# State-space steps between the projections: TensorE in the order of the source, two heads alternating on the column halves

## The chip, the cores and the metric

One core of a Trainium2 chip runs the kernel. The metric is the device time of one execution in microseconds; the median of three runs is given. TensorE does the matmuls, VectorE and ScalarE the elementwise work, SyncE issues the loads and stores. GpSimd does nothing here.

## What is computed

One layer of a hybrid block on 256 latent tokens and 256 context tokens of width 2048, in fp32. A normalised and modulated input goes through one wide projection. Its columns feed a state-space mixer (SSD: 32 heads of 64 in 4 groups, state 128, chunks of 128 tokens, both directions), a recurrent mixer (RG-LRU) and gates; an output projection and a gated FFN follow. The change touches the state-space mixer:

```python
def ssd_scan(x, dt, A, B, C, h0):
    xdt, Bc, a_cum, states, chunk_decay = _ssd_chunks(x, dt, A, B)
    entering, final = _carry_states(states, chunk_decay, h0)
    ...
    Lmat = jnp.exp(jnp.where(lower, seg, -jnp.inf))
    CB = jnp.einsum('bcign,bcjgn->bcijg', Cc, Bc)
    y_diag = jnp.einsum('bcijg,bcijge,bcjgep->bcigep', CB, Lmat, xdt)
    y_off = jnp.einsum('bcign,bcige,bcgepn->bcigep', Cc, jnp.exp(a_cum), entering)
    return (y_diag + y_off).reshape(b_, L, G, E, P), final
```

It is done forward and backward and summed; the context gives the states that enter the latent scan. Then `y * silu(z)`, a norm and the projection `w_out_ssd`.

## The kernel before

A *job* is one projection of 128 output columns: its weight comes in parts of 8 k-tiles (512 KB each, `load`), ScalarE rounds a part to `wh`, VectorE takes the rest `wl = raw - wh` (`parts`, L165 and L166), and `product` (L171 on) accumulates `wh` and `wl` against the split activations in one of three PSUM banks named `ps`. "both" jobs cover latent and context tokens (three matmuls of 512 columns per k-tile, 48 in all, L177 to L179), "lat" jobs the latent tokens (48 of 256 columns, L181 to L183), "packed" jobs two matmuls per k-tile (512 and 256 columns, L195 and L196). Four buffers each of raw weights, `wh` and `wl` go round, and `forward` keeps them filled. After its last matmul a job calls `evac`, whose first step is a ScalarE copy out of `ps` (L393, L426, L256).

`run` walks through a list of jobs. After each it issues one step of `ada_rest` (two loads of 512 KB and a VectorE product each, L415 and L416), where there are some, and takes one or two entries off the queue `bg` and calls them.

The list `jobs` has first the step sizes, the recurrent mixer's projections and gates (34 jobs), then for each of four groups B, C and four x projections (`bs_evac`, `cs_evac`, `xs_evac`: a convolution over four taps on ScalarE and VectorE), then eight gate jobs. Sixteen z jobs and sixteen yr jobs follow. When a group's last x is there, `ssd_group(g)` puts ten entries on `bg`: the three Silus; `products` (transposes pB of B into Bt, and pC = B.C, masked into U and L); transposes px of x with weighted copies xw; context states (p0); carried states (p1); and four units (u, c), each four heads on one chunk of 128 tokens. A unit loads AC, makes the operands E, G and CE on ScalarE and VectorE, and then does for each pair of heads t and each head e of the pair three matmuls py with 64 weight columns (L742 to L744): head e = 0 writes PSUM partitions 0 to 63, e = 1 partitions 64 to 127. `dve` adds the skip term into yt (L746), and y goes to DRAM for the z jobs. State-space PSUM tiles come from three banks named `ssd`; two more, `lru`, belong to the recurrent mixer and a few sums.

The order of the instructions on each engine is set by a planner that simulates the program and takes what is ready by priority. Only the first stage fixes TensorE's and SyncE's order by hand. So around the groups TensorE's matmuls of different jobs and of the state-space steps stand as the planner mixed them. An fp32 matmul shows as two passes in the records.

Of the kernel before, what the change touches and what calls it, by code (L numbers as in the profile page):

```python
# [14 lines left out]
P = 128  # L15
# [39 lines left out]
def hybrid_block(  # L55
# [152 lines left out]
    bg, loaded, n_parts = deque(), deque(), [0]  # L208

    def run(jobs, after=(), ada=(), every=1, start=0):  # L210
# [54 lines left out]
    def rstd_of(ps, n, name):  # L265
        r = tp.tile([P, n], F32, tag="rstd", name=name, bufs=1)
        fn(r, ps[:, :n], AF.Sqrt, bias=epsb[:, 0:1], scale=1.0 / D)
        dve.reciprocal(r, r)
        return r
# [14 lines left out]
    r1 = rstd_of(ssq, 2 * T, "r1")  # L284
# [311 lines left out]
    def start_ssd():  # L596
# [6 lines left out]
        held["ld"] = ap_stack.enter_context(tc.tile_pool(name="ld", bufs=5))  # L603
# [3 lines left out]
    def bs_evac(g):  # L607
        def f(ps):
            if g == 0:
                start_ssd()  # L610
            gp = sd["gp"]
            B = sd["B"] = gp.tile([P, 2 * T], F32, tag="B", name="B", bufs=1)
            conv(ps, B.rearrange("p (s t) -> p s t", s=2), col("cw", 4 * (16 + g), 4), col("cb", 16 + g), 2)
        return f

    def cs_evac(g):
        def f(ps):
            gp = sd["gp"]
            Cm = sd["C"] = gp.tile([P, T], F32, tag="C", name="Cm", bufs=2)
            conv(ps, Cm.unsqueeze(1), col("cw", 4 * (20 + g), 4), col("cb", 20 + g), 1)  # L620
            sd["XS"] = gp.tile([P, 4, 2 * T], F32, tag="XS", name="XS", bufs=2)
        return f

    def xs_evac(g, t):
        def f(ps):
            i = 4 * g + t
            conv(ps, sd["XS"][:, t, :].rearrange("p (s t) -> p s t", s=2), col("cw", 4 * i, 4), col("cb", i), 2)
            if t == 3:
                bg.extend(ssd_group(g))
        return f  # L630

    def ssd_group(g):
# [15 lines left out]
        def products():  # L648

            pb = ssd_ps("pB")  # L650
            for q in range(4):
                pe.transpose(pb[:, q * P:q * P + P], B[:, q * P:q * P + P], ident)
            Bt = st["Bt"] = gp.tile([P, 4, P], F32, tag="Bt", name="Bt")
            act.copy(Bt.rearrange("p a b -> p (a b)"), pb)

            pc = ssd_ps("pC")
# [9 lines left out]
        def tokens(qs):  # L666

            def weighted(ps, blk, d):
                o = gp.tile([P, 4 * P], F32, tag="xw", name="xw", bufs=3)
                dve.tensor_tensor(heads(o), heads(ps), head_scale(wt[:, blk], d), ALU.mult)  # L670
                return o

            def f():
                for q in qs:
                    px = ssd_ps("px")
                    for t in range(4):
                        pe.transpose(px[:, t * P:t * P + P], XS[:, t, q * P:q * P + P], ident)
                    if q < 2:
                        o = st["xt", q] = gp.tile([P, 4 * P], F32, tag="xt", name="xt", bufs=2)
                        act.copy(o, px)  # L680
                        st["xl", q] = weighted(px, 4, q)
                    else:
                        for d in range(2):
                            st["xc", d, q - 2] = weighted(px, 3 + q, d)
            return f

        def context_states():
            for d in range(2):
                p0 = ssd_ps("p0")
# [5 lines left out]
                st["S", d, d] = s0  # L695

        def carried_states():
            for d in range(2):
                p1 = ssd_ps("p1")
                pe.matmul(p1, st["Bt"][:, d, :], st["xl", d], start=True, stop=True)  # L700
                s1 = gp.tile([P, 4 * P], F32, tag="s1", name="s1", bufs=2)
                dve.tensor_tensor(heads(s1), heads(st["S", d, d]), head_scale(dec, d), ALU.mult)
                dve.tensor_tensor(s1, p1, s1, ALU.add)
                st["S", 1 - d, d] = s1

        def unit(u, c):

            def f():
                if c == 0:
                    for t in range(2):  # L710
                        st["y", t] = gp.tile([P, T], F32, tag="yt", name="yt", bufs=2)
                U, L = st["U"], st["L"]
                h0 = 8 * g + 4 * u
                cs = slice(c * P, c * P + P)
                AC = gp.tile([P, 2, 4, P], F32, tag="AC", name="AC", bufs=2)
                side.dma_start(AC.rearrange("p d h i -> p d (h i)"),
                                    acD[c, :, h0:h0 + 4, :].rearrange("d h i -> d (h i)").partition_broadcast(P))
                CE = gp.tile([P, 2, 4, P], F32, tag="CE", name="CE", bufs=1)
                fn(CE, AC, AF.Exp)
                CEv = CE.rearrange("p d h i -> p (d h) i")  # L720
                dve.tensor_tensor(CEv, CEv, Cm[:, cs].unsqueeze(1).broadcast_to([P, 8, P]), ALU.mult)
                E = gp.tile([P, 4, P], F32, tag="E", name="E", bufs=1)
                G = gp.tile([P, 4, P], F32, tag="G", name="G", bufs=1)
                for h in range(4):
# [3 lines left out]
                                             ALU.add, ALU.min)  # L728
                fn(E, E, AF.Exp)
                for h in range(4):  # L730
# [4 lines left out]
                dve.tensor_tensor(G, G, E, ALU.mult)  # L735
                for t in range(2):
                    py = ssd_ps("py")
                    for e in range(2):
                        h = 2 * t + e
                        xs = slice((4 * u + h) * 64, (4 * u + h) * 64 + 64)  # L740
                        o = py[64 * e:64 * e + 64, :P]
                        pe.matmul(o, st["xt", c][:, xs], G[:, h], start=True, stop=False)  # L742
                        pe.matmul(o, st["S", c, 0][:, xs], CE[:, 0, h], start=False, stop=False)
                        pe.matmul(o, st["S", c, 1][:, xs], CE[:, 1, h], start=False, stop=True)  # L744
                    i = 4 * g + 2 * u + t
                    dve.scalar_tensor_tensor(st["y", t][:, cs], XS[:, 2 * u + t, cs], col("dsk", i), py[:, :P],  # L746
                                             ALU.mult, ALU.add)
                    if c:
                        side.dma_start(yD[i], st["y", t])
            return f  # L750

        return ([silus, products, tokens((2, 3)), context_states, tokens((0, 1)), carried_states]
                + [unit(u, c) for u in range(2) for c in range(2)])

# [4 lines left out]
    jobs += gates_next(6)  # L759
    for g in range(NG):  # L760
        jobs.append(Job(w_bc[g], KT, "both", None, bs_evac(g)))
        jobs.append(Job(w_bc[4 + g], KT, "lat", None, cs_evac(g)))
        for t in range(4):
            jobs.append(Job(w_xs[4 * g + t], KT, "both", None, xs_evac(g, t)))
# [59 lines left out]
    run(jobs, after=z_jobs, ada=range(26), start=39)  # L824


    for k in range(KT):
        dve.tensor_copy(T1[:, k, T:], T2[:, k, :T].bitcast(F32))

    run(z_jobs, after=yr_jobs)  # L830
# [185 lines left out]
```

## Time and profile before

| | |
|---|---|
| median of three runs | 2035.52 us (2035.03 to 2035.86) |
| the profiled execution's own time | 2039.19 us |
| its span | 2037.4 us |
| TensorE matmuls busy | 1997.7 us, 98% |
| VectorE / ScalarE busy | 1436.5 us, 71% / 1084.1 us, 53% |
| mean granted TensorE clock | 0.994 of 2.4 GHz |
| HBM traffic | 438 MB, 215 GB/s over the span |

Matmuls are pipelined and their ends are modelled, so how long TensorE takes for something is read from the starts: the distance from one start to the next. In the rows below a timeline row is: start in us, length in us, engine, line, operation, output <- inputs, shapes and number of merged instructions; in square brackets what the engine waited for just before. Group 0 of the state-space work has its last projection at 496 us, the gate jobs begin near 737, the z jobs near 805, the yr jobs near 911.

### The profile page before, as it was taken

The page shows a single profiled execution, that of the slowest core. Times are in us where ns is not written, and L with a number is a line of the kernel's source. Part 1 is how long each engine was busy: PE and PEld are TensorE (multiplying, and loading weights), DVE is VectorE, ACT ScalarE, POOL GpSimd, SP SyncE. Part 2 cuts the span into 40 slices and gives each one's busy share as a digit, 9 for nine tenths or more (in the row PEclk, how much of TensorE's full clock was granted, in tenths as well). Part 3 has the DMA queues.
Part 4 walks back from the last instruction along what each step waited for, and adds up shares of the span by engine and source line. Part 5 has one row for each costly group of instructions (what it writes and reads, how often), then busy time and mean ns, then how long its engine had stood idle before and what let it go on. Part 6 is the DMA issues. An engine that isn't in the chain of part 4 may idle for free.

```text
span 2037.4 us, 30480 instructions
## 1 busy us (share of the span) xinstructions
PE 1997.7 (98%) x11633; PEld 1692.2 (83%) x11633; DVE 1436.5 (71%) x2148; ACT 1084.1 (53%) x1644; POOL 0.2 (0%) x4
## 2 busy tenths in 40 slices
PE   7999999999999999999999999999999999999997
PEld 4679888898777788888888888788888888888886
DVE  5467899985777788879896666766666665545554
ACT  4344888874453545755655544544444444544442
POOL 0000000000000000000000000000000000000000
PEclk9999999999999999999999999999999999999999
DMA  9984445464565668699996655577767765566663
GB/s 359 356 275 147 136 137 158 150 201 144 185 194 175 199 197 283 187 351 328 322 344 214 193 193 188 169 225 241 235 231 227 237 220 185 182 190 187 186 192 124
DMA packets 143266, 440.32 MB, mean 216 GB/s; under 512 B 17424, under 2 KB 36112, under 8 KB 142992
## 3 DMA queue, kind: packets, MB, share of 16 engines
q1 hardware_dynamic: 142752, 437.91, 66.2%
q8 instruction: 91, 1.49, 0.3%
q10 hardware_dynamic: 368, 0.47, 0.1%
q14 instruction: 55, 0.45, 0.1%
HBM read 427.77 MB, written 10.55 MB: 215 GB/s over the span
## 4 chain that ended last, share of the span: by engine, by line
PE 89%; DMA 4%; ACT 3%; DVE 2%; issue 1%; DVEq 0%; SPq 0%; ACTq 0%
PE ps L195 37%; PE ps L196 19%; PE ps L177 5%; PE ps L178 5%; PE ps L179 5%; PE ps L181 3%; PE ps L182 3%; PE ps L183 3%; DMA raw<-in_dram 1%; PE ps L342 1%; PE ps L343 1%; PE ps L344 1%; PE pa L295 1%; DMA wa<-in_dram 1%; DMA X<-in_dram 1%
## 5 line engine op out<-in xcount | busy, mean ns | idle before, releaser
L195 PE MATMUL ps<-T,wh 128*128 128x512 f32 x3332 | 1174.0, 397 | 7.0 <-DVE T L924 4.5
L166 DVE TENSOR_TENSOR wl<-raw,wh 128x1024 fp32r<-128x1024 f32 (+1 forms) x562 | 678.2, 1208 | 391.7 <-ACT wh L165 388.6
L165 ACT CAST wh<-raw 128x1024 fp32r<-128x1024 f32 (+1 forms) x562 | 582.0, 1038 | 677.8 <-issue 277.1
L196 PE MATMUL ps<-T,wl 128*128 128x256 f32 x3332 | 935.4, 281 | 0.8 <-DVE wl L166 0.8
L195 PEld LDWEIGHTS ps<-T,wh 128*128 128x128 f32 x3332 | 626.0, 188 | 158.8 <-issue 5.3
L196 PEld LDWEIGHTS ps<-T,wl 128*128 128x128 f32 x3332 | 629.6, 189 | 2.8 <-DVE wl L166 1.3
L416 DVE SCALAR_TENSOR_TENSOR rawa<-rawa,sc 128x1024 f32<-128x1024 f32 x128 | 156.5, 1222 | 76.6 <-DMA rawa<-in_dram 75.7
L177 PE MATMUL ps<-T,wh 128*128 128x512 f32 x464 | 186.0, 401 | 0.4 <-ACT gt L426 0.4
L178 PE MATMUL ps<-T,wh 128*128 128x512 f32 x464 | 185.2, 399 | 0.0
L179 PE MATMUL ps<-T,wl 128*128 128x512 f32 x464 | 184.2, 397 | 0.0
L182 PE MATMUL ps<-T,wh 128*128 128x256 f32 x576 | 165.4, 287 | 0.0
L183 PE MATMUL ps<-T,wl 128*128 128x256 f32 x576 | 164.8, 286 | 0.0
L181 PE MATMUL ps<-T,wh 128*128 128x256 f32 x576 | 164.3, 285 | 0.4 <-ACT gt L426 0.4
L181 PEld LDWEIGHTS ps<-T,wh 128*128 128x128 f32 x576 | 110.8, 192 | 4.2 <-issue 1.5
L183 PEld LDWEIGHTS ps<-T,wl 128*128 128x128 f32 x576 | 110.9, 193 | 2.8 <-issue 1.9
L182 PEld LDWEIGHTS ps<-T,wh 128*128 128x128 f32 x576 | 111.0, 193 | 2.6 <-issue 1.2
L177 PEld LDWEIGHTS ps<-T,wh 128*128 128x128 f32 x464 | 87.2, 188 | 22.8 <-issue 4.9
L179 PEld LDWEIGHTS ps<-T,wl 128*128 128x128 f32 x464 | 87.1, 188 | 21.5 <-issue 4.0
L178 PEld LDWEIGHTS ps<-T,wh 128*128 128x128 f32 x464 | 87.2, 188 | 21.4 <-issue 4.7
L106 ACT ACT_TABLE_LOAD x44 | 56.5, 1283 | 0.7
L336 DVE TENSOR_TENSOR wl<-raw,wh 128x896 fp32r<-128x896 f32 x16 | 17.5, 1092 | 45.7 <-ACT wh L335 45.7
L342 PE MATMUL ps<-T,wh 128*128 128x512 f32 x112 | 47.4, 423 | 0.0
(234 smaller groups left out, 1833.4 us busy)
## 6 DMA issues: line engine op xcount, KB each, us to landing
raw<-in_dram SPq DMA_DIRECT2D x546, 512.0 KB, 4.5
rawa<-in_dram SPq DMA_DIRECT2D x128, 512.0 KB, 4.8
wa<-in_dram SPq DMA_DIRECT2D x64, 512.0 KB, 7.6
AC<-acD SPq DMA_DIRECT2D x16, 512.0 KB, 6.2
raw<-in_dram SPq DMA_DIRECT2D x16, 448.0 KB, 7.9
raw<-in_dram SPq DMA_DIRECT2D x18, 256.0 KB, 2.7
X<-in_dram SPq DMA_DIRECT2D x8, 512.0 KB, 7.2
lw<-in_dram SPq DMA_DIRECT2D x16, 256.0 KB, 3.4
```

The costliest lines, as they stand in the source:

```text
L165: act.copy(h[:, :n], raw[:, :n])
L166: dve.tensor_sub(l[:, :n], raw[:, :n], h[:, :n].bitcast(F32))
L177: pe.matmul(ps, wh, T1[:, k, :], start=s, stop=False)
L178: pe.matmul(ps, wh, T2[:, k, :], start=False, stop=False)
L179: pe.matmul(ps, wl, T1[:, k, :], start=False, stop=e)
L181: pe.matmul(ps[:, :T], wh, T1[:, k, :T], start=s, stop=False)
L182: pe.matmul(ps[:, :T], wh, T2[:, k, :T], start=False, stop=False)
L183: pe.matmul(ps[:, :T], wl, T1[:, k, :T], start=False, stop=e)
L195: pe.matmul(ps, wh, a, start=s, stop=False, skip_group_check=True)
L196: pe.matmul(ps[:, T:], wl, a[:, :T], start=False, stop=e, skip_group_check=True)
L342: pe.matmul(ps0[n], h[:, n, :], T1[:, k, :], start=k == 0, stop=False)
L416: dve.scalar_tensor_tensor(rv, rv, 1.0, sc[:, h * 1024:h * 1024 + 1024], ALU.mult, ALU.mult, accum_out=MP[:, n, h:h + 1])
```

## The change

- TensorE's instructions from the first group's first job to the last z job stand in the order of the source (`manual_schedule` for PE). All other engines stay under the planner.
- A group's steps no longer queue in `bg`. Each gets a turn: `in_turn(n, f)` calls f after the n-th job from the group's last x on (that job is turn 0). For groups 0 to 2: Silus at 0; context_tokens, context_states, carried_states at 1, 2, 3; the units' operands at 3 to 6 and their products at 4 to 7. For the last group, among gate and z jobs: 0; 2, 3, 5; 5, 7, 9, 11; 7, 9, 11, 13. Operands and products of a unit are two steps.
- The transposes of x and their weighted copies are split over context_tokens and context_states, each with eight transposes in a row; both p1 are issued together.
- A unit's twelve products go to one PSUM bank, the two heads of a pair taking turns: first term of head 0, of head 1, second term of head 0, and so on.
- The state-space tiles go round over five banks (three `ssd`, two `lru`).
- The projections of a group come in the order x, C, x, B, x, x. The pools open at the first x.
- CE is made in place in AC (three buffers, not two), E and G share three buffers, the `ld` ring has four tiles, not five, and the first norm's `r1` lies in another pool.

```diff
+    banks = deque((ssd_ps, lru_ps, ssd_ps, lru_ps, ssd_ps))
+
+    def bank(name):
+        banks.rotate(-1)
+        return banks[-1](name)
...
-            for _ in range(2 if len(bg) > 7 else 1):
-                if bg:
-                    with tc.high_priority(0):
+            with tc.high_priority(0):
+                for f in turns.popleft() if turns else ():
+                    f()
+                for _ in range(2 if len(bg) > 7 else 1):
+                    if bg:
                         bg.popleft()()
...
-        held["ld"] = ap_stack.enter_context(tc.tile_pool(name="ld", bufs=5))
+        held["ld"] = ap_stack.enter_context(tc.tile_pool(name="ld", bufs=4))
...
+    LONG = ((0,), (1, 2, 3), (3, 4, 5, 6), (4, 5, 6, 7))
+    SHORT = ((0,), (2, 3, 5), (5, 7, 9, 11), (7, 9, 11, 13))
...
             if t == 3:
-                bg.extend(ssd_group(g))
+                for ns, fs in zip(LONG if g < NG - 1 else SHORT, ssd_group(g)):
+                    for n, part in zip(ns, fs):
+                        in_turn(n, part)
...
+        def tokens(q):
+
+            px = bank("px")
+            for t in range(4):
+                pe.transpose(px[:, t * P:t * P + P], XS[:, t, q * P:q * P + P], ident)
+            return px
+
+        def context_tokens():
...
+            px = [tokens(2), tokens(3)]
+            Bt = st["Bt"] = gp.tile([P, 4, P], F32, tag="Bt", name="Bt")
+            act.copy(Bt.rearrange("p a b -> p (a b)"), pb)
...
+            for i in range(2):
+                for d in range(2):
+                    st["xc", d, i] = weighted(px[i], 5 + i, d)
...
         def context_states():
+            px = [tokens(0), tokens(1)]
             for d in range(2):
-                p0 = ssd_ps("p0")
+                p0 = bank("p0")
...
+                py = bank("py")
                 for t in range(2):
-                    py = ssd_ps("py")
-                    for e in range(2):
-                        h = 2 * t + e
-                        xs = slice((4 * u + h) * 64, (4 * u + h) * 64 + 64)
-                        o = py[64 * e:64 * e + 64, :P]
-                        pe.matmul(o, st["xt", c][:, xs], G[:, h], start=True, stop=False)
-                        pe.matmul(o, st["S", c, 0][:, xs], CE[:, 0, h], start=False, stop=False)
-                        pe.matmul(o, st["S", c, 1][:, xs], CE[:, 1, h], start=False, stop=True)
+
+                    for n in range(3):
+                        for e in range(2):
+                            h = 2 * t + e
+                            xs = slice((4 * u + h) * 64, (4 * u + h) * 64 + 64)
+                            w, m = ((st["xt", c], G[:, h]), (st["S", c, 0], CE[:, 0, h]),
+                                    (st["S", c, 1], CE[:, 1, h]))[n]
+                            pe.matmul(py[64 * e:64 * e + 64, t * P:t * P + P], w[:, xs], m,
+                                      start=n == 0, stop=n == 2, skip_group_check=True)
...
-    run(jobs, after=z_jobs, ada=range(26), start=39)
...
+    run(jobs[:n_lru], after=jobs[n_lru:])
+    with tc.manual_schedule(engines={mybir.EngineType.PE}):
+        run(jobs[n_lru:], after=z_jobs, ada=range(26), start=39 - n_lru)
...
+        run(z_jobs, after=yr_jobs)
```

## Rows read from the trace of the kernel before

**Rows 1.** Table by stage: span, engines' busy us (instructions), TensorE clock, DMA share, GB/s.

```profile
578.00:660.00 82.00, 82.00 (x399) 61.53 (x398) 60.40 (x102) 39.62 (x65) 0.00 (x0) 1.00 0.57 184
738.00:805.00 67.00, 64.22 (x497) 58.65 (x496) 54.76 (x97) 39.07 (x67) 0.00 (x0) 0.95 0.84 265
...
911.00:1000.00 89.00, 89.00 (x505) 77.16 (x504) 79.81 (x126) 50.31 (x82) 0.00 (x0) 1.00 0.94 327
```

**Rows 2.** TensorE's waits, 440 to 900 us: us in total, times, longest.

```profile
PE pC L659 <- ACT Bt L654: 2.8, 1, 2.8
PE ps L195 <- ACT wh L165: 1.6, 2, 1.4
```

**Rows 3.** ScalarE's timeline: copies that drain projections, at the ends of stages.

```profile
486.49 0.58 ACT L393 COPY pad<-ps 128x512 f32<-128x512 f32 x1
...
497.37 0.58 ACT L393 COPY pad<-ps 128x512 f32<-128x512 f32 x1
...
738.12 0.58 ACT L393 COPY pad<-ps 128x512 f32<-128x512 f32 x1
...
805.54 0.38 ACT L426 COPY gt<-ps 128x256 f32<-128x256 f32 x1
...
911.09 0.37 ACT L256 COPY zt<-ps 128x256 f32<-128x256 f32 x1 [0.70 <-PE ps L196]
```

**Rows 4.** TensorE's timeline around its longest wait in the stage.

```profile
788.05 0.28 PE L183 MATMUL ps<-T,wl 128*128 128x256 f32 x1
788.17 0.28 PE L181 MATMUL ps<-T,wh 128*128 128x256 f32 x1
791.23 1.22 PE L659 MATMUL pC<-Cm,B 128*128 128x128 f32 x4 [2.78 <-ACT Bt L654]
...
796.73 0.41 PE L183 MATMUL ps<-T,wl 128*128 128x256 f32 x1
796.94 0.41 PE L181 MATMUL ps<-T,wh 128*128 128x256 f32 x1
```

**Rows 5.** TensorE's timeline: full-array state-space passes among packed projections.

```profile
807.10 1.02 PE L691 MATMUL p<-xw,Bt 128*128 128x512 f32 x2
807.95 0.60 PE L677 MATMUL px<-K,XS 128*128 128x128 f32 x4
808.31 0.36 PE L196 MATMUL ps<-T,wl 128*128 128x256 f32 x1
808.51 0.40 PE L195 MATMUL ps<-T,wh 128*128 128x512 f32 x1
```

**Rows 6.** Groups of TensorE instructions, 497 to 911 us: count, busy us, mean ns.

```profile
L742 PE MATMUL py<-G,xt 128*64 128x128 f32 x128 | 24.3, 290 | 0.0
...
L677 PE MATMUL px<-K,XS 128*128 128x128 f32 x64 | 11.4, 291 | 0.0
L690 PE MATMUL p<-xw,Bt 128*128 128x512 f32 x16 | 8.3, 598 | 0.5 <-DVE xw L670 0.5
```

**Rows 7.** TensorE's timeline: products that stand alone between projection matmuls.

```profile
548.05 0.39 PE L179 MATMUL ps<-T,wl 128*128 128x512 f32 x1
548.37 0.43 PE L742 MATMUL py<-G,xt 128*64 128x128 f32 x2
548.74 0.49 PE L177 MATMUL ps<-T,wh 128*128 128x512 f32 x1
549.16 0.43 PE L743 MATMUL py<-CE,s 128*64 128x128 f32 x2
```

**Rows 8.** TensorE's timeline: a unit's products in one block.

```profile
843.20 0.43 PE L742 MATMUL py<-G,xt 128*64 128x128 f32 x2
...
843.69 0.27 PE L744 MATMUL py<-CE,s 128*64 128x128 f32 x1
...
843.80 0.27 PE L744 MATMUL py<-CE,s 128*64 128x128 f32 x1
...
844.93 0.38 PE L196 MATMUL ps<-T,wl 128*128 128x256 f32 x1
```

More of the change, by code (lines that the diff above doesn't have):

```diff
@@ L208, in hybrid_block, with in_turn @@
     bg, loaded, n_parts = deque(), deque(), [0]
+    turns = deque()
+    def in_turn(n, f):
+        while len(turns) <= n:
+            turns.append([])
+        turns[n].append(f)
     def run(jobs, after=(), ada=(), every=1, start=0):
@@ L263, in split, with rstd_of @@
         dve.tensor_sub(dst[:, T:], src, dst[:, :T].bitcast(F32))
-    def rstd_of(ps, n, name):
-        r = tp.tile([P, n], F32, tag="rstd", name=name, bufs=1)
+    def rstd_of(ps, n, name, pool=tp):
+        r = pool.tile([P, n], F32, tag="rstd", name=name, bufs=1)
         fn(r, ps[:, :n], AF.Sqrt, bias=epsb[:, 0:1], scale=1.0 / D)
@@ L283, in hybrid_block @@
         pe.matmul(ssq, ones, sq[:, 0], start=k == 0, stop=k == KT - 2)
-    r1 = rstd_of(ssq, 2 * T, "r1")
+    r1 = rstd_of(ssq, 2 * T, "r1", sp)
     ras = {}
@@ L608, in f @@
         def f(ps):
[L609 to L612, printed above, removed]
+            B = sd["B"] = sd["gp"].tile([P, 2 * T], F32, tag="B", name="B", bufs=1)
             conv(ps, B.rearrange("p (s t) -> p s t", s=2), col("cw", 4 * (16 + g), 4), col("cb", 16 + g), 2)
@@ L617, in f @@
         def f(ps):
-            gp = sd["gp"]
-            Cm = sd["C"] = gp.tile([P, T], F32, tag="C", name="Cm", bufs=2)
+            Cm = sd["C"] = sd["gp"].tile([P, T], F32, tag="C", name="Cm", bufs=2)
             conv(ps, Cm.unsqueeze(1), col("cw", 4 * (20 + g), 4), col("cb", 20 + g), 1)
-            sd["XS"] = gp.tile([P, 4, 2 * T], F32, tag="XS", name="XS", bufs=2)
         return f
+    LONG = ((0,), (1, 2, 3), (3, 4, 5, 6), (4, 5, 6, 7))
+    SHORT = ((0,), (2, 3, 5), (5, 7, 9, 11), (7, 9, 11, 13))
     def xs_evac(g, t):
         def f(ps):
+            if (g, t) == (0, 0):
+                start_ssd()
+            if t == 0:
+                sd["XS"] = sd["gp"].tile([P, 4, 2 * T], F32, tag="XS", name="XS", bufs=2)
             i = 4 * g + t
@@ L646, in silus, with weighted @@
                 fn(t, t, AF.Silu)
-        def products():
-            pb = ssd_ps("pB")
+        def weighted(ps, blk, d):
+            o = gp.tile([P, 4 * P], F32, tag="xw", name="xw", bufs=3)
+            dve.tensor_tensor(heads(o), heads(ps), head_scale(wt[:, blk], d), ALU.mult)
+            return o
+        def tokens(q):
[4 more added lines that the diff above has]
+        def context_tokens():
+            pb = bank("pB")
             for q in range(4):
                 pe.transpose(pb[:, q * P:q * P + P], B[:, q * P:q * P + P], ident)
-            Bt = st["Bt"] = gp.tile([P, 4, P], F32, tag="Bt", name="Bt")
-            act.copy(Bt.rearrange("p a b -> p (a b)"), pb)
-            pc = ssd_ps("pC")
+            pc = bank("pC")
             for c in range(2):
@@ L664, in products @@
             dve.tensor_tensor(L, pcv, mL.unsqueeze(1).broadcast_to([P, 2, P]), ALU.mult)
[L666 to L685, printed above, removed]
         def context_states():
+            px = [tokens(0), tokens(1)]
             for d in range(2):
-                p0 = ssd_ps("p0")
+                p0 = bank("p0")
                 pe.matmul(p0, st["Bt"][:, 2, :], st["xc", d, 0], start=True, stop=False)
@@ L695, in context_states, with operands @@
                 st["S", d, d] = s0
+            for q in range(2):
+                o = st["xt", q] = gp.tile([P, 4 * P], F32, tag="xt", name="xt", bufs=2)
+                act.copy(o, px[q])
+                st["xl", q] = weighted(px[q], 4, q)
         def carried_states():
+            ps = []
             for d in range(2):
-                p1 = ssd_ps("p1")
+                p1 = bank("p1")
                 pe.matmul(p1, st["Bt"][:, d, :], st["xl", d], start=True, stop=True)
+                ps.append(p1)
+            for d in range(2):
                 s1 = gp.tile([P, 4 * P], F32, tag="s1", name="s1", bufs=2)
                 dve.tensor_tensor(heads(s1), heads(st["S", d, d]), head_scale(dec, d), ALU.mult)
-                dve.tensor_tensor(s1, p1, s1, ALU.add)
+                dve.tensor_tensor(s1, ps[d], s1, ALU.add)
                 st["S", 1 - d, d] = s1
         def unit(u, c):
[L708 to L711, printed above, removed]
+            h0 = 8 * g + 4 * u
+            cs = slice(c * P, c * P + P)
+            def operands():
                 U, L = st["U"], st["L"]
-                h0 = 8 * g + 4 * u
-                cs = slice(c * P, c * P + P)
-                AC = gp.tile([P, 2, 4, P], F32, tag="AC", name="AC", bufs=2)
+                AC = gp.tile([P, 2, 4, P], F32, tag="AC", name="AC", bufs=3)
                 side.dma_start(AC.rearrange("p d h i -> p d (h i)"),
                                     acD[c, :, h0:h0 + 4, :].rearrange("d h i -> d (h i)").partition_broadcast(P))
[L718 to L723, printed above, removed]
+                E = gp.tile([P, 4, P], F32, tag="E", name="E", bufs=3)
+                G = gp.tile([P, 4, P], F32, tag="E", name="G", bufs=3)
                 for h in range(4):
@@ L728, in f @@
                                              ALU.add, ALU.min)
+                fn(AC, AC, AF.Exp)
                 fn(E, E, AF.Exp)
+                ACv = AC.rearrange("p d h i -> p (d h) i")
+                dve.tensor_tensor(ACv, ACv, Cm[:, cs].unsqueeze(1).broadcast_to([P, 8, P]), ALU.mult)
                 for h in range(4):
@@ new lines, in products @@
+            def products():
+                if c == 0:
+                    for t in range(2):
+                        st["y", t] = gp.tile([P, T], F32, tag="yt", name="yt", bufs=2)
+                G, CE = st.pop(("u", u, c))
+                py = bank("py")
+                for t in range(2):
+                    for n in range(3):
[6 more added lines that the diff above has]
+                                      start=n == 0, stop=n == 2, skip_group_check=True)
+                for t in range(2):
@@ L752, in ssd_group @@
-        return ([silus, products, tokens((2, 3)), context_states, tokens((0, 1)), carried_states]
-                + [unit(u, c) for u in range(2) for c in range(2)])
+            return operands, products
+        units = [unit(u, c) for u in range(2) for c in range(2)]
+        return ([silus], [context_tokens, context_states, carried_states],
+                [o for o, _ in units], [p for _, p in units])
     jobs = [Job(w_dt, KT, "narrow", None, dt_evac)]
@@ L759, in hybrid_block @@
     jobs += gates_next(6)
+    n_lru = len(jobs)
     for g in range(NG):
[L761 to L764, printed above, removed]
+        group = [Job(w_xs[4 * g + t], KT, "both", None, xs_evac(g, t)) for t in range(4)]
+        group[2:2] = [Job(w_bc[g], KT, "both", None, bs_evac(g))]
+        group[1:1] = [Job(w_bc[4 + g], KT, "lat", None, cs_evac(g))]
+        jobs += group
     jobs += [gate_job(n) for n in ng]
@@ L822, in hybrid_block @@
     yr_jobs = [yr_job(i) for i in range(KT)]
-    run(jobs, after=z_jobs, ada=range(26), start=39)
-    for k in range(KT):
-        dve.tensor_copy(T1[:, k, T:], T2[:, k, :T].bitcast(F32))
-    run(z_jobs, after=yr_jobs)
+    run(jobs[:n_lru], after=jobs[n_lru:])
+    with tc.manual_schedule(engines={mybir.EngineType.PE}):
+        run(jobs[n_lru:], after=z_jobs, ada=range(26), start=39 - n_lru)
+        for k in range(KT):
+            dve.tensor_copy(T1[:, k, T:], T2[:, k, :T].bitcast(F32))
+        run(z_jobs, after=yr_jobs)
+    assert not turns
     rs1 = total_rstd(sq1, "rs1")
```

6 lines of the change are left out of this document (3 added, 3 removed).

## The prediction

> **What bounds the kernel now.** I read the table by stage first: in a group's stretch TensorE counts as busy in all 82 of 82 us [rows 1]. So a change can gain only by giving TensorE less to do, or by making what it does cheaper; waits hold little. In the list of TensorE's waits, cut to the stage that changes, the two longest entries come to 2.8 and 1.6 us [rows 2]. That would leave nothing to win if "busy" meant "at its peak". It doesn't: the ends of matmuls are modelled, so the next view is the distance between starts.
>
> To see what the state-space work costs, I take the ScalarE copies that drain a projection's PSUM bank as milestones [rows 3]. Two neighbours without state-space work between them stand 497.37 - 486.49 = 10.88 us apart: one "both" projection (48 matmuls). A "lat" projection is 48 starts 0.12 us apart [rows 4], 5.76 us. A "packed" one: 505 matmuls in 89 us, 32 to a job, so 5.64 us [rows 1]. From the end of group 0's projections on [rows 3]:
> - groups 1 to 3, 497.37 to 738.12: 240.75 us, projections 3 x (5 x 10.88 + 5.76) = 180.5, over: 60.3;
> - eight gate jobs, to 805.54: 67.42 us, projections 8 x 5.76 = 46.1, over: 21.3;
> - sixteen z jobs, to 911.09: 105.55 us, projections 16 x 5.64 = 90.2, over: 15.3.
>
> So the state-space work of four groups adds **96.9 us** to TensorE's path. Of that, 2.8 and 1.6 are waits [rows 2], and some 3.1 are a slow clock: after the 2.8 us wait TensorE went on at 1.2 GHz, with 0.21 us between starts in place of 0.12 [rows 4]; a granted clock of 0.95 in the mean of 67 us [rows 1] is half clock for 6.7 us and a loss of some 3.1 to 3.3. That leaves 96.9 - 7.5 = **89.4 us** of matmuls and of what switching to them costs.
>
> **The change, part by part.**
>
> *Full-array steps (pB, pC, px, p0, p1).* Same instructions, same shapes. Each 512-column pass takes 0.428 us (807.10 to 807.95 is two). Four px and the projection matmul behind them take 807.95 to 808.51, 0.56; less that matmul's 0.12 it is 0.11 for a 128-column pass [rows 5]. There are 64 px and, at four per group, 16 pB and 16 pC; p0 and p1 are three lines of 16 [rows 4, 6]: 96 x 0.11 + 48 x 0.428 = 31.1 us. Before, many stand singly between projection matmuls, but in [rows 5] entering and leaving cost next to nothing, so packing them gives nothing I count. Twelve whole steps with 0.1 us each to enter: 1.2.
>
> *Products (py).* Three lines of 128 passes: 192 fp32 products of two passes [rows 6]. They use half the array's columns. A lone one between projection matmuls is dear: 548.37 to 549.16 is one product and one projection matmul, 0.79 us; less the projection's 0.227 (10.88 / 48), 0.56 per product [rows 7]. Where the planner happened to put products of both column halves side by side, two passes start every 0.11 us, one on each half (843.69 to 843.80, with one of the other half left out between them), so 0.055 a pass [rows 8]. All in all the 192 cost 89.4 - 31.1 - 1.2 = 57.1 us, 0.30 each: a mixture of the two. After the change all twelve products of a unit stand together and the halves alternate from the first. One unit: 24 x 0.055 = 1.31, plus 0.09 to enter (0.32 from the last projection matmul to the product, not 0.227 [rows 7]), and an estimated 0.1 each for the first pass, which has no partner, and for leaving: 1.6 us. The nearest whole block before takes 843.20 to 844.93 = 1.73 and its entry, 1.82, because its halves are shifted against each other [rows 8]. Bounds 1.5 to 1.82; I take 1.6. Sixteen units: 25.6 us (24.0 to 29.1).
>
> Sum after: 31.1 + 1.2 + 25.6 = 57.9 us (56.3 to 61.4) in place of 89.4: **31.5 us less work** (28.0 to 33.1).
>
> *TensorE in the order of the source.* This removes the planner's freedom to fill a wait with matmuls of another job. From now on, whatever stands behind a late step waits with it: the next projection first, then the weight ring that it would free, then SyncE's loads. Where a step may be late: the px of group g follow one projection after the last x, 10.9 us, in which come pad copy, convolution and a Silu over 2048 columns; p0 comes one "lat" projection (5.8 us) after px, and needs VectorE's weighted copies and the bank that U and L read. There are only three xw buffers for the four weighted tiles of the context, so the fourth waits on VectorE for p0's first matmuls, with weight splits queued behind it. The units have it easier: their operands are issued one projection (10.9 us) or two short ones before the products, and AC, E and G now have three buffers each. VectorE is busy 60.4 of 82 us in a group [rows 1]; with the same work in 60.2 + 14 us that is 81%. In the gate stage 54.8 of 67 us [rows 1] becomes 54.8 of some 57: next to full, but its ada halves needn't be there. In the row where TensorE never waited, VectorE was at 79.8 of 89 us, 90% [rows 1]. Bounds: no wait at all (gain 7.5 more), or a wait in each of the 28 steps. I take the 7.5 us that before has, clock and all, because the steps have more lead than the work needs and only the gate stage is tight.
>
> *Loads.* SyncE's queue stays under the planner, and past it move only the units' own AC loads and y stores, sixteen of each, with three AC buffers in place of two to be early; POOL has nothing to be moved past. The weights and the 26 ada steps are the same, and so is the job at which ada begins (39 - 34 = 5 in the new count). The gate stage moved 265 GB/s over 67 us [rows 1]; in 57 us the same bytes are 311 GB/s, under the 327 of the stage after z [rows 1]: nothing, or up to 5 us if that is a limit for it too.
>
> *The rest.* The order x, C, x, B, x, x permutes equal jobs, and splitting the run in two and moving r1 to another pool leave the work as it is. The ld ring of four in place of five covers four z jobs, 22 us; CE in AC's place makes one exponential wait for eight small reads ahead of it, with a projection of lead; one py bank for a unit and five banks in turn only move who waits for PSUM. All nothing while TensorE has other work, which it has.
>
> **Forecast.** 31.5 us off the profiled execution's own 2039.2 us (span 2037.4 and 1.8 around it) is 2007.7; the median of the runs stands 3.7 us under that execution, so **2004 us**. With the bounds of the work (28.0 to 33.1) and of the waits (none, or 7.5 more): 1995 to 2015.
>
> **Rivals.**
> 1. *VectorE or the loads set the pace of part of the stage.* For: 54.8 of 57 us in the gate stage, and three xw buffers. Against: 90% with no wait after z. Price: waits of 20 to 32 us in all in place of 7.5, so gains of 19 to 7: 2016 to 2028.
> 2. *Slower: late steps cost the clock as well.* The wait in [rows 4] was 2.8 us and took 3.1 more at 1.2 GHz, 5.9 in all. If px and p0 of all four groups are late like that, it is 8 x 5.9 = 47 us, against 31.5 + 7.5 = 39.0 that can be gained: 2044 us. It decides from the seventh such wait on, or from 1.4 us at each of 28 steps. For: that wait was at exactly such a step (pC behind Bt), and in order nothing fills it. Against: it happened once at 28 steps. The Trainium skill, "TensorE: Matmul & The Clock Gate", Part 1, says that the half rate is the default and only activity lifts it; by that rule every long wait pays twice, as [rows 4] shows for the one there is.
> 3. *The change doesn't do what it says:* halves in turn but not side by side. Then a pass takes 0.109, a unit 2.9 us, the sixteen 46.4: 20.8 us of the gain go, 2025 us. Against: the block in [rows 8], 24 passes in 1.73 us, can't be had at 0.109 a pass (2.6).
>
> **Chances.** Forecast 0.60, better than it (under 1995) 0.04, rival 1 0.18, rival 3 0.04, the gain gone to within 0.2% (2031.4 to 2039.6) 0.05, rival 2 0.09. The range, 1995 to 2028, holds 0.82 and leaves out the slower end and the luckiest. A measurement of this kernel can't tell less than about 0.2% from no change: faster 0.86, same 0.05, slower 0.09.
>
> **What would show it.** After: py passes 0.055 us apart in blocks of 24, sixteen of them, none alone; three groups in about 225 us between the copies that now stand at 497.37 and 738.12, the gate and z jobs in about 155 us from there; projections at the old paces. Wrong would be: TensorE waits of more than 15 us in the stage; clock rows of 0.5 beside them; blocks whose passes stand 0.109 apart; or a stage after z that has grown because its loads were pushed back.

## The result, and the profile after

The changed kernel takes **2048.0 us** (median of 8 runs, 2042.1 to 2053.6) where the kernel before, on the same chip, takes 2034.9: a ratio of **1.0076, 95% interval 1.0053 to 1.0100**. It is slower. The forecast was 2004 us with a range to 2028, and faster with 0.86: wrong in sign, and the time lies 20 us outside the range. The profiled execution took 2049.1 us (span 2047.3), 9.9 us more than that of before.

The same milestones as in [rows 3] come first: ScalarE's copies at the end of group 0's projections, of group 3's and of the z jobs.

```profile
495.26 0.58 ACT L409 COPY pad<-ps 128x512 f32<-128x512 f32 x1
...
750.96 0.57 ACT L409 COPY pad<-ps 128x512 f32<-128x512 f32 x1
...
922.63 0.37 ACT L272 COPY zt<-ps 128x256 f32<-128x256 f32 x1 [1.35 <-PE ps L203]
```

From the first to the last it is 427.4 us, in [rows 3] 413.7: 13.7 us more. The stage begins 2.1 us earlier and what lies behind it is 1.6 us shorter, which gives the 9.9. All of the loss is in the stage that the change touches; 316.8 us of it are projections at their old paces, so the state-space work now adds 110.6 us, not 96.9, and not the 65.4 of the forecast.

Next the table by stage (us, busy us and instructions of PE, PEld, DVE, ACT and POOL, granted clock, DMA share, GB/s): the whole stage, then the stage after it.

```profile
494.00:923.00 429.00, 389.54 (x2296) 323.40 (x2295) 326.98 (x575) 228.69 (x390) 0.00 (x0) 0.96 0.67 214
...
922.00:1010.00 88.00, 88.00 (x508) 77.56 (x507) 79.41 (x126) 50.93 (x82) 0.00 (x0) 1.00 0.94 333
```

TensorE, which [rows 1] shows busy in 82 of 82 us of a group, is now idle in 39 of 429, and its clock has fallen to 0.96 in the mean. The stage after z is as it was, 333 GB/s and no idle time. The list of TensorE's waits in the stage, which held 2.8 and 1.6 us at its head in [rows 2], names the place:

```profile
PE p L709 <- DVE xw L672: 32.5, 4, 11.6
PE ps L203 <- DVE wl L173: 2.4, 4, 0.8
PE py L774 <- DVE G L757: 1.6, 1, 1.6
PE px L679 <- DVE yt L778: 1.4, 1, 1.4
PE ps L202 <- ACT wh L172: 1.4, 2, 1.1
```

32.5 of 39.3 us are one wait, once in each group: the second direction of the context states (p0) for its weighted copy xw. TensorE's timeline around the longest of the four:

```profile
595.39 1.06 PE L679 MATMUL px<-K,XS 128*128 128x128 f32 x8 [1.41 <-DVE yt L778]
596.56 1.12 PE L708 MATMUL p<-xw,Bt 128*128 128x512 f32 x2
597.75 1.12 PE L709 MATMUL p<-xw,Bt 128*128 128x512 f32 x2
598.72 1.02 PE L708 MATMUL p<-xw,Bt 128*128 128x512 f32 x2
611.36 2.07 PE L709 MATMUL p<-xw,Bt 128*128 128x512 f32 x2 [11.62 <-DVE xw L672]
612.45 1.42 PE L184 MATMUL ps<-T,wh 128*128 128x512 f32 x1
```

And VectorE's over the same time:

```profile
595.82 1.88 DVE L672 TENSOR_TENSOR xw<-px,wt 128x512 f32<-128x512 f32 x3
...
598.28 1.13 DVE L755 SCALAR_TENSOR_TENSOR G<-L,wt,G 128x128 f32<-128x128 f32 x4
...
604.75 1.23 DVE L432 SCALAR_TENSOR_TENSOR rawa<-rawa,sc 128x1024 f32<-128x1024 f32 x1 [4.81 <-DMA rawa<-in_dram]
...
609.49 1.22 DVE L173 TENSOR_TENSOR wl<-raw,wh 128x1024 fp32r<-128x1024 f32 x1
610.62 0.68 DVE L672 TENSOR_TENSOR xw<-px,wt 128x512 f32<-128x512 f32 x1
```

Three of the four copies are made in a row. The fourth needs the buffer that p0's first matmuls free when they end (596.56 and 1.12, some 597.7); it starts at 610.62. Between stand fifteen other VectorE instructions, one of them an ada product whose 512 KB load has not landed: 4.81 us in which VectorE stands still with everything behind it. And VectorE comes to the copies late: it starts the first at 595.82, 0.7 us before p0's first matmul, and the px just ahead of p0 has itself waited 1.41 us for VectorE (595.39). The Trainium skill, "PSUM — Partial Sum Buffer", Engine vs sequencer instructions, says that VectorE's queue is strictly first in, first out; these rows agree, since from some 597.7 on the fourth copy lacked nothing but its turn. The load itself was issued at 594.75 by SyncE's timeline, behind two weight loads and an AC load, and landed 10.0 us later, where the median of this tile's loads in the kernel is 4.9.

TensorE, in the order of the source, has nothing else it may do. It pays for the clock too (table by stage, same columns, around this wait):

```profile
603.00:611.00 8.00, 0.00 (x0) 0.00 (x0) 6.25 (x10) 3.70 (x8) 0.00 (x0) 0.53 0.43 137
611.00:617.00 6.00, 5.64 (x11) 3.81 (x12) 6.00 (x13) 0.58 (x1) 0.00 (x0) 0.50 0.67 211
617.00:622.00 5.00, 5.00 (x23) 4.05 (x22) 3.08 (x6) 1.50 (x3) 0.00 (x0) 0.99 0.31 93
```

The granted clock fell to 1.2 GHz while TensorE stood, and stayed there for the first six us of work. The clock rows of the stage at half rate are 3.4, 13.7, 10.2, 6.8 and 3.4 us long (37.5 in all; before it was 6.8); about 21 us of them are work, which cost some 10.6 us.

Last, one of the sixteen blocks of products, with its neighbours:

```profile
584.48 0.39 PE L186 MATMUL ps<-T,wl 128*128 128x512 f32 x1
584.80 0.44 PE L774 MATMUL py<-G,xt 128*64 128x128 f32 x4
585.07 0.60 PE L774 MATMUL py<-AC,s 128*64 128x128 f32 x8
585.50 0.39 PE L774 MATMUL py<-G,xt 128*64 128x128 f32 x4
585.72 0.60 PE L774 MATMUL py<-AC,s 128*64 128x128 f32 x8
586.26 0.66 PE L686 MATMUL pB<-K,B 128*128 128x128 f32 x4
```

24 passes in 1.46 us (584.80 to 586.26); the eight from 585.07 to 585.50 stand 0.054 us apart. With its entry (584.48 to 584.80 is 0.32, 0.09 over the 0.227 of a projection matmul) a block costs 1.55. That part of the change does what the prediction said. TensorE's timeline of the kernel before shows where it saves: nine of the sixteen units stood as whole blocks of 24 passes there already, 1.73 us each, and six were scattered, most of their products alone, for 5.5 to 6.1 us each over the projections between them.

### The profile page after: what moved, and what is told of

It reads as the page before. It is cut to its first block, busy times and chain, and to the rows that moved or that the text cites. A ratio compares the mean times of both kernels' runs of the same rounds, so it can differ in the third digit from the quotient of the medians.

```text
span 2047.3 us, 30483 instructions
## 1 busy us (share of the span) xinstructions
PE 1973.7 (96%) x11633; PEld 1685.0 (82%) x11633; DVE 1435.0 (70%) x2148; ACT 1086.5 (53%) x1646; POOL 0.2 (0%) x4
## 4 chain that ended last, share of the span: by engine, by line
PE 82%; DMA 8%; DVE 4%; ACT 3%; issue 2%; SPq 0%; DVEq 0%; ACTq 0%
PE ps L202 37%; PE ps L203 19%; DMA rawa<-in_dram 6%; PE ps L184 4%; PE ps L185 4%; PE ps L186 3%; PE ps L188 2%; PE ps L189 2%; PE ps L190 2%; DVE wl L173 1%; PE ps L358 1%; PE pa L311 1%; PE ps L359 1%; PE ps L360 1%; DMA raw<-in_dram 1%
## 5 line engine op out<-in xcount | busy, mean ns | idle before, releaser
L432 DVE SCALAR_TENSOR_TENSOR rawa<-rawa,sc 128x1024 f32<-128x1024 f32 x128 | 156.3, 1222 | 94.1 <-DMA rawa<-in_dram 93.5
```

What stands on the lines that cost most here:

```text
L432: dve.scalar_tensor_tensor(rv, rv, 1.0, sc[:, h * 1024:h * 1024 + 1024], ALU.mult, ALU.mult, accum_out=MP[:, n, h:h + 1])
```

## The experiments

The theory from this profile: the change saves the work that was forecast, and loses more at one crossing, where TensorE waits in order for VectorE. Open was which of three things makes that wait: the number of xw buffers (A), VectorE's ada steps and their loads (B), or the fixed order of TensorE as such (C). In the table, "adds" is the length of the stage between ScalarE's copies, as above, less the 316.8 us of projections (before is 96.9 and after 110.6); "p0" is TensorE's wait at p0, "half" the clock rows at half rate in the stage, all of the profiled execution. "Ratio" is to the kernel before, run beside it.

| kernel | median us | ratio, 95% | adds | p0 | half |
|---|---|---|---|---|---|
| own slot for the fourth xw | 2033.3 | 0.9997 (0.9979 to 1.0014) | 94.8 | 0 | 20.5 |
| after, no ada steps in the stage | 2000.0 (one run) | | 61.2 | 1.3 | 0 |
| after, TensorE under the planner | 2066.4 | 1.0162 (1.0136 to 1.0188) | 128.1 | 0 | 0 |
| own slot, heads in sequence | 2034.0 | 0.9993 (0.9973 to 1.0013) | 99.2 | 0 | 20.5 |
| before, no ada steps in the stage | 2027.6 | 0.9955 (0.9928 to 0.9982) | 91.2 | | 0 |
| after, ada products without their loads | 2007.8 (two runs) | 0.9864 (0.9808 to 0.9920) | 74.7 | 10.2 | 10.2 |
| after, ada loads with small products | 2028.1 | 0.9963 (0.9941 to 0.9984) | 92.1 | 22.0 | 27.3 |
| after, ada thinned | 2007.8 | 0.9860 (0.9825 to 0.9895) | 76.1 | 10.0 | 10.2 |
| own slot and ada thinned | **1998.9** | **0.9826 (0.9788 to 0.9863)** | 59.0 | 0 | 0 |
| before, ada thinned | 2032.1 | 0.9995 (0.9983 to 1.0007) | 94.1 | | 0 |

**The fourth copy in a slot of its own.** The copy for the second direction and second block goes to a tile that is free by then; nothing else changes.

```diff
-        def weighted(ps, blk, d):
-            o = gp.tile([P, 4 * P], F32, tag="xw", name="xw", bufs=3)
+        def weighted(ps, blk, d, tag="xw", bufs=3):
+            o = gp.tile([P, 4 * P], F32, tag=tag, name="xw", bufs=bufs)
...
-                    st["xc", d, i] = weighted(px[i], 5 + i, d)
+                    st["xc", d, i] = weighted(px[i], 5 + i, d, *(("s1", 2) if d and i else ()))
```

> The changed kernel with one thing different: the fourth weighted tile of the context (xc of direction 1, second half) takes a slot of the s1 tiles, which lie idle then, in place of the third xw buffer, so that VectorE needn't wait for p0's first matmuls to make it. Theory A (the fourth tile has no buffer until TensorE has begun p0, so it stands on VectorE behind some ten other instructions, and TensorE in order stands still until it comes): the waits of p0 for xw, 32.5 us in four, fall to under 3 us, the 37.5 us of half clock in the stage to under 10, and the time to 1995 to 2008 us. Rival B (VectorE and the ada loads are simply too slow for a stage this short): the waits move to the next step that is late, their sum stays over 20 us and the time over 2025 us.

Measured: 2033.3 us. The 32.5 us at p0 are gone, as A said, and the time is not where A put it. The head of TensorE's list of waits in the stage:

```profile
PE ps L190 <- DVE wl L173: 6.6, 4, 3.2
PE px L679 <- ACT XS L106: 4.9, 3, 3.0
PE px L679 <- DVE yt L778: 4.4, 2, 3.1
PE ps L203 <- DVE wl L173: 3.1, 4, 1.0
PE ps L202 <- ACT wh L172: 2.2, 3, 1.2
```

The waits have moved, as B said, to what VectorE and ScalarE make next: 21.2 us in these rows, in pieces up to 3.2 us, with 20.5 us at half clock. So few buffers are the place of the wait, worth 15 us, but not all of its cause.

**No ada steps in the stage.** The run through the group, gate and z jobs issues none; `dve.memset` fills the two tables that they would have filled.

```diff
-        run(jobs[n_lru:], after=z_jobs, ada=range(26), start=39 - n_lru)
+        run(jobs[n_lru:], after=z_jobs, ada=(), start=39 - n_lru)
```

> The changed kernel without the 26 ada steps in this stage: their loads and VectorE products are left out (a part of the second modulation is then not computed). Three xw buffers as in the changed kernel. Theory A: TensorE still waits at p0's second direction in all four groups, since the fourth tile still has no buffer until p0 has begun; each wait is shorter by what the ada products in front of it took (up to 4.8 us of load wait and 2.3 us of work), 2 to 6 us each. Rival B (loads and VectorE's load): with 26 MB and 60 us of VectorE work gone, the waits go altogether, under 3 us in the stage.

Measured: 2000.0 us, with the three xw buffers of the change:

```profile
PE p L711 <- DVE xw L674: 1.3, 1, 1.3
```

A's wait in each group doesn't appear: without the ada steps three buffers are enough. B is right, and the state-space work adds 61.2 us with no half clock: this is the change without nearly all of its waits. Its queue shows why. In the same group as above fourteen instructions, 6.9 us, stand between the third copy and the fourth here too (VectorE, then p0's start on TensorE):

```profile
584.12 1.88 DVE L674 TENSOR_TENSOR xw<-px,wt 128x512 f32<-128x512 f32 x3
...
592.87 0.69 DVE L674 TENSOR_TENSOR xw<-px,wt 128x512 f32<-128x512 f32 x1
```

```profile
590.73 1.02 PE L710 MATMUL p<-xw,Bt 128*128 128x512 f32 x2
```

But VectorE starts the copies 6.6 us before p0, not 0.7, and works most of that queue off meanwhile. Over the four groups its lead is 5.5 to 6.6 us here, 24.2 in all, and 0.7 to 2.8 in the change, 6.9 in all. So the ada steps lengthen p0's waits in two ways: some 17 us are lead that VectorE has lost before it reaches the copies, and some 15 are what they put between the third copy and the fourth, 9.5 of them standing still for loads.

**TensorE under the planner again**, all else as in the change.

```diff
-    with tc.manual_schedule(engines={mybir.EngineType.PE}):
+    with ExitStack():
```

> The changed kernel with TensorE given back to the planner: everything else (turns, alternating heads, five banks, buffers) stays. Theory A: the planner fills the wait for the fourth tile with other matmuls, so p0's waits fall under 5 us; but it mixes products with projections again, so that the state-space work costs 75 to 95 us more than the projections as before, not the 60 or so of whole blocks: 2020 to 2040 us. Rival C (the order of the source as such is what costs, wherever it waits): the products stay cheap and the time is 1995 to 2010 us.

Measured: 2066.4 us, worse than either theory said. There is no wait over a microsecond, but the planner scatters the products; TensorE's timeline:

```profile
591.38 0.39 PE L186 MATMUL ps<-T,wl 128*128 128x512 f32 x1
591.70 0.43 PE L774 MATMUL py<-G,xt 128*64 128x128 f32 x2
592.06 0.38 PE L188 MATMUL ps<-T,wh 128*128 128x256 f32 x1
592.38 0.43 PE L774 MATMUL py<-G,xt 128*64 128x128 f32 x2
592.74 0.39 PE L189 MATMUL ps<-T,wh 128*128 128x256 f32 x1
```

A product and a projection matmul take 0.68 us; less the 0.12 of the projection it is 0.56 each, just what [rows 7] gave for a lone one. With the new order of the source and a free planner, more products stand alone than before: 154 runs of a single product, 53 in the kernel before. The fixed order is what makes the blocks; it can't be dropped to get rid of the waits.

**The heads in sequence**, on top of the own slot: first the three products of one head, then those of the other.

```diff
-                    for n in range(3):
-                        for e in range(2):
+                    for e in range(2):
+                        for n in range(3):
```

> As e1_own_slot, but a unit's heads one after the other (all three terms of head 0, then of head 1) in the same block. If alternation is what puts two passes side by side, the passes of a unit stand 0.109 us apart and the 16 units cost 16 x 24 x 0.055 = 21 us more than in e1_own_slot. If TensorE overlaps the halves whatever the order within a block, as the whole blocks of the kernel before hint at, the difference is under 6 us.

Measured: 2034.0 us, 0.7 above the own slot, a difference within the intervals; the stage adds 99.2 us, 4.4 more. One block, from TensorE's timeline:

```profile
568.45 0.43 PE L774 MATMUL py<-G,xt 128*64 128x128 f32 x2
568.72 0.27 PE L774 MATMUL py<-AC,s 128*64 128x128 f32 x1
568.73 0.32 PE L774 MATMUL py<-G,xt 128*64 128x128 f32 x1
...
569.59 0.66 PE L774 MATMUL py<-AC,s 128*64 128x128 f32 x6
570.18 0.50 PE L184 MATMUL ps<-T,wh 128*128 128x512 f32 x1
```

The block takes 1.73 us in place of 1.46, as the shifted block in [rows 8] did. Passes of both heads lie within each other all the same: head 1's first product starts at 568.73, between the passes of head 0's second, though in the order of the source it stands behind all three of head 0's. So the second theory holds and standing together is what pays; by the trace the alternation adds 0.27 us a block, 4.3 in all, too little for the medians to show.

**The kernel before without ada steps in the stage.**

> The kernel before without the 26 ada steps of this stage (left out; a part of the second modulation is then not computed). Theory A2 (the change makes the state-space work on TensorE some 30 us cheaper, as priced, and the ada steps take it back only because TensorE in order can't work around VectorE's waits for their loads): the kernel before hid the ada steps behind other matmuls, so without them it gains little more than its own waits, 5 to 12 us, to 2022 to 2030 us, and stays 25 us or more above the changed kernel without ada (2000.0 us). Rival B2 (the ada steps cost both kernels alike): it falls by 30 us or more, to under 2006 us, and the cheaper products are worth little.

Measured: 2027.6 us, 27.6 above the change without them. That is what A2 said. In the old order the ada steps cost some 8 us (2035.3, run beside it, less 2027.6), in the new one some 48 (2048.0 less the one run of 2000.0). VectorE waits for their loads in both; the head of its list of waits in the stage, in the kernel before and in the change:

```profile
DVE rawa L416 <- DMA rawa<-in_dram: 44.9, 30, 2.6
```

```profile
DVE rawa L432 <- DMA rawa<-in_dram: 61.7, 33, 4.8
```

**Which half of an ada step.** First the products without the loads, then the loads with products over 16 columns:

```diff
+            sh = sc[:, h * 1024:h * 1024 + 1024]
+            if n >= 26:
+                nc.sync.dma_start(rv, w_ada_r[n, :, h * 1024:h * 1024 + 1024])
+            dve.scalar_tensor_tensor(rv, sh if n < 26 else rv, 1.0, sh, ALU.mult, ALU.mult,
...
+            m = 16 if n < 26 else 1024
+            dve.scalar_tensor_tensor(rv[:, :m], rv[:, :m], 1.0, sc[:, h * 1024:h * 1024 + m], ALU.mult, ALU.mult,
```

> The changed kernel with the 26 ada steps' VectorE products kept, each of full length and with its raw buffer, but without their loads: they read the resident row sc twice (that part of the modulation is then not what it should be). If VectorE's waits for these loads, 59 us in the stage, are what makes p0's fourth tile late, p0's waits fall from 32.5 us to under 10 and the time to 2000 to 2015 us. If VectorE's amount of work does it, the waits stay over 20 us and the time over 2030 us.

> The other half: the changed kernel with all ada loads, and VectorE still waiting for each, but the product on 16 columns in place of 1024 (0.1 us, not 1.2; the sums are then not what they should be). If the waits for the loads are the cause, p0's waits stay over 15 us and the time over 2025 us. If the work is, they fall under 10 us and the time to 2000 to 2015 us.

Measured: 2007.8 and 2028.1 us. The p0 rows of the two lists of waits, products first:

```profile
PE p L711 <- DVE xw L674: 10.2, 4, 3.2
```

```profile
PE p L710 <- DVE xw L673: 22.0, 4, 10.8
```

Together 32.2 us, near the 32.5 of the change. The loads hold up p0 more, some 22 us, and VectorE's work some 10; both time and wait of the second are as the expectation had it for the loads, and the wait of the first is just over its bound of 10. These are single profiled executions, the two runs of the first are 12 us apart (2001.9 and 2013.8), and leaving out the loads takes their traffic away too, so the split is a rough one.

**The ada steps thinned.** Every second projection of the stage gets one, 13 in all; the other 13 are done in the three later runs of projections. Nothing is left out. It is tried in the change, in the own slot's kernel and in the kernel before.

```diff
-        run(jobs[n_lru:], after=z_jobs, ada=range(26), start=39 - n_lru)
+        run(jobs[n_lru:], after=z_jobs, ada=range(13), every=2, start=39 - n_lru)
...
-    run(yr_jobs, after=mixj, ada=range(26, 32), every=2)
+    run(yr_jobs, after=mixj, ada=range(13, 29))
...
-    run(mixj[:2 * KT], after=mixj[2 * KT:], ada=range(32, 42), every=3)
+    run(mixj[:2 * KT], after=mixj[2 * KT:], ada=range(29, 45), every=2)
...
-    run(mixj[2 * KT:], after=ffnj, ada=range(42, 48), every=2)
+    run(mixj[2 * KT:], after=ffnj, ada=range(45, 48), every=2)
```

> The changed kernel with half as many steps of the adaptive weights inside the state-space stage (one at every second projection, 13 steps; the other 13 go to the later stages), and with the three xw buffers of the changed kernel. The own-slot kernel with the same thinning took 1998.9 us and had TensorE wait for 0.8 us in the stage. Theory A (three buffers for four weighted tiles is by itself a cause: VectorE can make the fourth only after the first matmuls of p0, and some ten instructions stand before it): p0 still waits 2 to 6 us in each of the four groups, 8 to 25 us in all, and parts of the half clock come back, so 2008 to 2025 us. Theory B (the few buffers only matter where an adaptive step stands on VectorE between the third tile and the fourth): with one at every second projection it stands there in one group or two, so waits of 0 to 5 us and 1997 to 2005 us.

> e1_own_slot with half of the ada steps moved out of the stage: 13 of them there, one after every second job, 16 with the yr jobs, 16 with the next 32 jobs, three with the w_o jobs; nothing left out. Theory A2: the stage's waits fall under 12 us and the time to 2000 to 2012 us, as long as the later stage, whose loads stood at 327 GB/s, hides the 13 it gets. Rival: it doesn't, its weights come late, and the time stays within 10 us of the kernel before.

> The kernel before the change with the same thinning of the adaptive weights (13 steps in the stage, 13 later), nothing left out. It tells what the whole steps and the column halves are worth once the loads are out of the way. Theory A (the work saved is worth what the prediction worked out, 28 to 33 us, and thinning itself brings the old order only its 7 us of waits and slow clock): 2025 to 2032 us, 26 to 33 us above the thinned own-slot kernel's 1998.9. Theory B (the thinning itself is what made that kernel fast, whatever the order): 2000 to 2012 us.

Measured: 2007.8 us in the change (2001.0 to 2014.7; the profiled execution is the slowest), **1998.9 with the own slot, 1.7% under the kernel before**, and 2032.1 in the kernel before. The longest wait of the first and of the second:

```profile
PE p L709 <- DVE xw L672: 10.0, 4, 3.6
```

```profile
PE ps L203 <- DVE wl L173: 0.8, 3, 0.4
```

With thinning alone p0 still waits in all four groups of the profiled execution, as A said, and the median is at the lower edge of A's time; but two of the four runs (2001.0 and 2003.1) lie in B's, so it is not decided between the two. With both, TensorE waits for 0.8 us in 376. VectorE then makes all four copies in a row (one row of its timeline):

```profile
584.75 2.48 DVE L672 TENSOR_TENSOR xw<-px,wt 128x512 f32<-128x512 f32 x4
```

The kernel before gains nothing that can be told from thinning. So with half of the ada steps out of the way the change with the own slot is worth 2032.1 - 1998.9 = 33.2 us, and two causes hold it back. The ada steps are the larger: thinning saves 40 us with three buffers and 34 with the own slot. The buffers cost 15 us with all ada steps; once these are thinned the own slot saves 9 us in the medians, but the two intervals overlap, so that is not shown.

## Why the prediction was wrong

- **What bounds the kernel, and the work saved: right.** The 31.5 us of less work are there (89.4 less 58.2 is 31.2). The state-space work adds 59.0 us, 0.8 of it waits (own slot, thinned), where the forecast was 57.9 (56.3 to 61.4) and the old order has 89.4. A block took 1.55 us with its entry, forecast 1.6 (1.5 to 1.82). The stage of that kernel is 221.0 us for the three groups and 155 for gates and z, where the prediction asked for about 225 and 155; in the change as made it is 255.7 and 171.7.
- **The waits: the step that failed.** "I take the 7.5 us that before has, clock and all, because the steps have more lead than the work needs and only the gate stage is tight." It measured 39.3 us of waits and some 10.6 of clock, 50 in all. The sum nearly closes: 59.0 of work + 39.3 + 10.6 = 108.9, and 110.6 were counted; 1.7 us are not assigned. The prediction had named the very place, "only three xw buffers for the four weighted tiles of the context", and gave it no price. The lead that it counted on at p0, one "lat" projection of 5.8 us, was 0.7 to 2.8 us in the change: VectorE came to the copies late, and for the fourth it then still had to work off what is queued ahead of it, fifteen instructions in the longest of the four waits. Where VectorE came 5.5 to 6.6 us ahead (no ada steps), a queue of the same kind cost 1.3 us in all.
- **The ada steps: the second failure, and the root of the first.** The phrase "its ada halves needn't be there" treats an ada product as something VectorE can leave for later. It stands at a place in VectorE's queue and, when its load is late, holds all behind it. In the kernel before VectorE waits for these loads too, 44.9 us in the stage, and TensorE for 5.7 in all: the planner had other matmuls for it. The change left VectorE's work much as it was, with 61.7 us for these loads, and took that cover away. The mean share of VectorE, 81%, said nothing about this: its busy time in the stage rose by 3 us (323.6 to 327.0).
- **The loads: right in amount, wrong in kind.** The stage after z moves 333 GB/s without a wait, so the rate that the prediction feared, 311, is none to stop at; the gate stage never came to it (248 GB/s from 751 to 819 us). What counted was when a single load landed: the one before the longest wait 10.0 us after its issue, with AC and weights before it.
- **The rivals.** Rival 2 is nearest, 2044 us forecast and 2048.0 measured, given 0.09. Its mechanism held (late steps, nothing to fill them, the clock on top), its count didn't: four waits of 8.1 us in the mean at p0, not eight of 2.8 at px and p0, and its cause is rival 1's, VectorE and loads, whose price of 20 to 32 us for waits was near (39.3) but counted no clock. That 2044 came so close is luck: 8 x 5.9 = 47 us from the wrong places against 39.3 + 10.6. The rule of the Trainium skill named there ("TensorE: Matmul & The Clock Gate", Part 1: half rate is the default and activity lifts it) agrees with the rows at 603 to 622 us. Rival 3 is out: 0.054 us a pass.
- **The range** should have reached the slower side: the bound "a wait in each of the 28 steps" was named and then not used.

What stays open: why VectorE's order, made by the planner, has so much between the third and the fourth copy. It wasn't tried to fix VectorE's order by hand.

## What to carry to other kernels

When an engine's order is fixed and its feeders stay under a planner, price each crossing: list what stands on the feeder's queue between the buffer coming free and the instruction that makes the operand, loads included, and count buffers against the tiles that one step needs. Ask too how far ahead of the step the feeder will be when it comes to that queue; its mean busy share doesn't tell. Background work that waits for loads belongs in stages with slack (on another engine it was not tried); here the same 26 steps cost some 8 us in one order and some 48 in the other. Matmuls packed on column halves are worth the fixed order that keeps them in blocks (33 us here, with the rest of the change), once those crossings are clear.

## What was not expected of the hardware

- Two heads' passes overlap on the column halves in a block even when they are issued one head after the other (1.73 us against 1.46 for 24 passes), and their starts leave the order of the source (568.73). Twelve products that each stand alone among projection matmuls, at 0.56 us, would take 6.7; the scattered units of the kernel before cost 5.5 to 6.1.
- A wait is followed by half clock also where it is not the longest: 5.0 us between starts (515.7 to 520.7) were followed by 3.4 us at 1.2 GHz, 12.2 us by a clock that fell within the wait and 6 us more. In pieces of up to 3.2 us (own slot) 23 us of waits still brought 20.5 us of half clock.
